# Weight chunks whose low part is made by an adding DMA instead of VectorE

## The chip, the cores and the metric

One core of one Trainium2 chip runs the kernel. The metric is the device time of one execution in microseconds (us).

## The reference

The reference is a two-layer decoder trunk on 256 tokens of width 2048, all in float32. Nearly all of its arithmetic lies in products with weight matrices. Layer 0 mixes tokens by causal spatial gating in parallel with attention into 256 memory tokens, layer 1 by latent attention in parallel with the same memory attention; each layer ends in a gated feed-forward block:

```python
D_MODEL = 2048; SEQ = 256; D_FF = 5632
...
for l in range(DEPTH):                      # DEPTH = 2
    h = rmsnorm(x, g_mix[l])
    ...                                     # main (gating or latent attention), mo (memory attention)
    x = x + jnp.concatenate([main, mo], axis=-1) @ w_out[l]
    x = x + conv_ffn(rmsnorm(x, g_ffn[l]), w_ffn_up[l], conv_w[l], conv_b[l], w_ffn_down[l])
return rmsnorm(x, g_final)

def conv_ffn(h, w_up, cw, cb, w_down):
    a = h @ w_up                            # 2048 x 11264
    ...                                     # causal depthwise convolution of width 3
    gate, val = c[..., :D_FF], c[..., D_FF:]
    return (jax.nn.silu(gate) * val) @ w_down
```

## The kernel before, in words

Every weight is read once from memory and used once. To keep float32 accuracy with a faster matmul type, each operand is split into a high part, which is the value rounded to that type (`F32R`), and a low part, which is the value minus its high part. A product is then high by high plus high by low plus low by high.

The weights come in *chunks*. `chunk` (line 92 on) allocates three tiles of 128 x 1024 values: `raw` (five buffers), `whi` and `wlo` (three each). SP issues the load of `raw` (line 98). For a chunk without gains ACT copies `raw` to `whi` (line 117) and DVE subtracts: `wlo = raw - whi` (line 118). Chunks with a per-row gain take lines 122 and 123, and other shapes lines 105/106 and 113/114. A full chunk holds two blocks of 128 rows by 512 columns of the weight, 512 KB.

`gemm_fm` makes four output blocks of 128 channels at a time, each accumulated in a PSUM bank (`ps`, eight banks, so two GEMMs' worth). It goes through the contraction two blocks at a time, one chunk each: 16 blocks make eight chunks, numbered 0 to 7 here. `mm_fm` issues a chunk's matmuls: eight of 512 columns with `whi` as weights (line 140; the moving operand holds the high and the low part of 256 tokens side by side) and eight of 256 columns with `wlo` (line 144). Even chunks do the high ones first, odd chunks the low ones first.

After a GEMM come its evictions. In the feed-forward block each of the four output blocks goes through `join` (ACT copies half the bank to `cr`, line 200; DVE adds it, `js`, line 202), POOL multiplies by the row factor (`a`, line 549), ACT and DVE do the convolution (`c`, lines 552 to 554) and ACT the gate (line 562) or DVE and ACT the product and its split. The next GEMM runs on the other four banks meanwhile. In the down-projection and the output projection DVE adds the two halves to the residual (lines 507 and 508).

The feed-forward block works in three parts of 4, 4 and 3 groups of 512 channels; a group is one GEMM of eight chunks for the gate and one for the value, and a part ends with four GEMMs of the down-projection, of eight, eight and six chunks. The order of the instructions on each engine is set when the program is built, by a scheduler that models a timeline; at run time each engine works through its own list in order and waits on semaphores.

Of the kernel before, what the change touches and what calls it, by code (L numbers as in the profile page):

```python
# [8 lines left out]
F32 = mybir.dt.float32  # L9
F32R = mybir.dt.float32r  # L10
I32 = mybir.dt.int32
BF16 = mybir.dt.bfloat16
AF = mybir.ActivationFunctionType
ALU = mybir.AluOpType
AX = mybir.AxisListType

P = 128
# [52 lines left out]
class Kernel:  # L70
# [18 lines left out]
        return pool.tile(shape, dt, tag=tag, name=self.uid(tag), bufs=bufs)  # L89


    def chunk(self, src, nk, ncol, gains=None, twice=False, heads=None):
        nc, n = self.nc, nk * ncol
        raw = self.wp.tile([P, 1024], F32, tag="raw", name=self.uid("raw"), bufs=5)
        hi = self.wp.tile([P, 1024], F32R, tag="whi", name=self.uid("whi"), bufs=3)
        lo = self.wp.tile([P, 1024], F32R, tag="wlo", name=self.uid("wlo"), bufs=3)
        view = lambda x: x[:, :n].rearrange("p (k c) -> p k c", k=nk)
        nc.sync.dma_start(out=view(raw), in_=src)
        if twice:
            both = lambda x: x.rearrange("p (k o c) -> p k o c", o=2, c=ncol)  # L100
            for k in range(nk):
                s = slice(k * ncol, (k + 1) * ncol)
                for o in range(2):
                    h = both(hi)[:, k, o, :]
                    nc.scalar.activation(h, raw[:, s], AF.Copy, scale=gains[k])
                    nc.vector.scalar_tensor_tensor(both(lo)[:, k, o, :], raw[:, s], gains[k], h.bitcast(F32), ALU.mult, ALU.subtract)  # L106
            return tuple(x.rearrange("p (k c) -> p k c", k=nk) for x in (hi, lo))
        if heads is not None:

            s = view(raw).rearrange("p k (h c) -> p k h c", h=2)  # L110
            for c0, c1 in ((0, heads), (heads, ncol // 2)):
                o = lambda x: view(x)[:, :, 2 * c0 : 2 * c1].rearrange("p k (h c) -> p k h c", h=2)
                nc.scalar.activation(o(hi), s[:, :, :, c0:c1], AF.Copy)
                nc.vector.tensor_tensor(o(lo), s[:, :, :, c0:c1], o(hi).bitcast(F32), ALU.subtract)
            return view(hi), view(lo)
        if gains is None:
            nc.scalar.activation(hi[:, :n], raw[:, :n], AF.Copy)  # L117
            nc.vector.tensor_tensor(lo[:, :n], raw[:, :n], hi[:, :n].bitcast(F32), ALU.subtract)  # L118
        else:
            for k in range(nk):  # L120
                s = slice(k * ncol, (k + 1) * ncol)
                nc.scalar.activation(hi[:, s], raw[:, s], AF.Copy, scale=gains[k])  # L122
                nc.vector.scalar_tensor_tensor(  # L123
                    lo[:, s], raw[:, s], gains[k], hi[:, s].bitcast(F32), ALU.mult, ALU.subtract
                )
        return view(hi), view(lo)
# [31 lines left out]
    def gemm_fm(self, src, kbs, nblk, rhs, evict, nk=2, gain=None, hooks={}):  # L158
        accs = [self.psum() for _ in range(nblk)]
        for c in range(0, len(kbs), nk):  # L160
            g = None if gain is None else [gain(kbs[c + i]) for i in range(nk)]
            hi, lo = self.chunk(src(kbs[c], nk), nk, nblk * P, g)
            jobs = []
            for b in range(nblk):
                cols = slice(b * P, (b + 1) * P)
                for i in range(nk):
                    kk = c + i
                    jobs.append((accs[b], hi[:, i, cols], lo[:, i, cols], rhs(kbs[kk]), kk == 0, kk == len(kbs) - 1))
            self.mm_fm(jobs, (c // nk) % 2)
            for f in hooks.get(c // nk, ()):  # L170
                f()
        for b in range(nblk):
            evict(b, accs[b])
# [135 lines left out]
    def gain(self, name, k):  # L309
        c = self.g[name] + k  # L310
        return self.gT[:, c : c + 1]
# [280 lines left out]
    def layer_a(self):  # L592
        nc, t, tc = self.nc, self.t, self.tc
# [3 lines left out]
        with ExitStack() as ctx:  # L597
# [25 lines left out]
            def spatial_weights():  # L623
                nc.sync.dma_start(out=bb, in_=t["b_sp"][0].rearrange("(o g) t -> o g t", o=1).to_broadcast([P, GH, P]))
                for g in range(0, GH, 4):
                    raw = self.wp.tile([P, 1024], F32, tag="raw", name=self.uid("raw"), bufs=5)
                    rv = raw[:, :512].rearrange("p (g s) -> p g s", g=4)
                    nc.sync.dma_start(out=rv, in_=t["w_sp"][0, g : g + 4].rearrange("g t s -> t g s"))
                    acc = self.psum()
                    for i in range(4):  # L630
                        nc.tensor.transpose(acc[:, i * P : (i + 1) * P], rv[:, i, :], self.ident)
                    for i in range(4):
                        nc.vector.tensor_tensor(wT[:, g + i, :], acc[:, i * P : (i + 1) * P], self.keep, ALU.mult)
# [329 lines left out]
```

## Time and profile before

| | |
|---|---|
| median of 2 runs | 2136.97 us (2136.78 to 2137.16) |
| the profiled execution | 2136.6 us, span 2134.5 us |
| mean granted TensorE clock | 0.997 |
| busy share of the span | PE 99%, PEld 87%, DVE 70%, ACT 54%, POOL 16% |
| DMA | 391 MB, 183 GB/s on average, 56.6% of 16 engines |

The span runs from the first to the last instruction of the profiled execution. PE is the matmul row and PEld the weight load that overlaps it; matmuls are pipelined and their ends are modelled, so a high share of PE doesn't say that it is at its peak. A line number names the line of the kernel that issued an instruction, and a tile is named by the program's name without its buffer number (`wlo`, `raw`). In the list of waits the columns are the waiting engine, tile and line, what ended the wait, the total in us, the number of waits and the longest.

### The profile page before, as it was taken

Reading aid. Unit: us, or ns where it says so; the run is one execution under the profiler, and the core shown is the slowest. Engines: PE = TensorE matmul, PEld = TensorE weight load, DVE = VectorE, ACT = ScalarE, POOL = GpSimd, SP = SyncE. Lnnn points to the kernel's source line nnn. Section 1 sums busy time; section 2 is a strip of 40 time slices with the busy share of each in tenths; the row PEclk is TensorE's granted clock in tenths of the full one; section 3 lists DMA queues with packets and bytes.
Section 4 is the critical chain, followed back from the end, with each engine's and each line's share of the span. In section 5 each row is a group of like instructions: output and inputs, shape, how many; then the busy total and the mean of one; then the engine's idle time right before and its main releaser. Section 6 shows DMA issues by size and latency. Waiting matters only on the chain.

```text
span 2134.5 us, 31965 instructions
## 1 busy us (share of the span) xinstructions
PE 2109.3 (99%) x11980; PEld 1847.7 (87%) x11980; DVE 1483.8 (70%) x2247; ACT 1151.5 (54%) x1800; POOL 338.3 (16%) x401
## 2 busy tenths in 40 slices
PE   8999999999999999999999999999999999999997
PEld 7888888888888888888888778888888888888886
DVE  6656667777656776667888775777765677656775
ACT  7654744656435564355556654465643556435554
POOL 0000124111001110011244111411100111001122
PEclk9999999999999999999999999999999999999998
DMA  8565455565555655566555523566555565556653
GB/s 280 179 206 183 154 193 188 188 194 182 196 188 188 191 184 194 187 190 190 186 188 164 155 97 129 188 188 194 182 196 188 188 191 184 196 187 189 189 187 109
DMA packets 208015, 391.02 MB, mean 183 GB/s; under 512 B 14366, under 2 KB 22900, under 8 KB 207860
## 3 DMA queue, kind: packets, MB, share of 16 engines
q1 hardware_dynamic: 207860, 388.98, 56.6%
q8 instruction: 94, 1.54, 0.3%
q14 instruction: 61, 0.50, 0.1%
HBM read 386.84 MB, written 2.10 MB: 182 GB/s over the span
## 4 chain that ended last, share of the span: by engine, by line
PE 97%; DVE 1%; ACT 1%; POOL 0%; DMA 0%; issue 0%; SPq 0%; ACTq 0%; DVEq 0%
PE ps L140 58%; PE ps L144 30%; PE ps L179 2%; PE ps L181 2%; PE ps L180 2%; PE ps L807 1%; PE ps L805 0%; PE ps L501 0%; PE ps L371 0%; PE ps L466 0%; PE ps L641 0%; DMA raw<-in_w_mem_kv 0%; DVE wlo L106 0%; PE ps L828 0%; PE ps L726 0%
## 5 line engine op out<-in xcount | busy, mean ns | idle before, releaser
L118 DVE TENSOR_TENSOR wlo<-raw,whi 128x1024 fp32r<-128x1024 f32 x660 | 820.6, 1245 | 484.7 <-ACT whi L117 480.6
L117 ACT ACTIVATE whi<-raw 128x1024 fp32r<-128x1024 f32 x660 | 697.6, 1057 | 647.6 <-PE ps L140 529.0
L140 PE MATMUL ps<-xhl,whi 128*128 128x512 f32 x3280 | 788.4, 391 | 1.6 <-ACT whi L122 1.6
L140 PEld LDWEIGHTS ps<-xhl,whi 128*128 128x128 f32 x3280 | 601.8, 188 | 117.4 <-ACT whi L122 1.8
L144 PEld LDWEIGHTS ps<-xhl,wlo 128*128 128x128 f32 x3280 | 422.9, 191 | 17.8 <-DVE wlo L106 0.7
L144 PE MATMUL ps<-xhl,wlo 128*128 128x256 f32 x3280 | 431.3, 283 | 0.2 <-DVE wlo L106 0.2
L549 POOL TENSOR_TENSOR a<-js,rbc 128x256 f32<-128x256 f32 x176 | 167.1, 960 | 1167.4 <-DVE js L202 1017.1
L140 PE MATMUL ps<-h,whi 128*128 128x512 f32 x1408 | 338.8, 391 | 0.0
L140 PEld LDWEIGHTS ps<-h,whi 128*128 128x128 f32 x1408 | 258.1, 188 | 49.5
L144 PEld LDWEIGHTS ps<-h,wlo 128*128 128x128 f32 x1408 | 181.4, 191 | 7.2
L144 PE MATMUL ps<-h,wlo 128*128 128x256 f32 x1408 | 184.7, 283 | 0.0
L552 ACT ACTIVATE c<-a,cT 128x256 f32<-128x256 f32 x176 | 99.9, 592 | 76.5 <-POOL a L549 76.5
L200 ACT ACTIVATE cr<-ps 128x256 f32<-128x256 f32 x243 | 91.0, 381 | 92.4 <-PE ps L140 83.4
L140 PE MATMUL ps<-mainhl,whi 128*128 128x512 f32 x512 | 122.7, 391 | 0.0
L202 DVE TENSOR_TENSOR js<-ps,cr 128x256 f32<-128x256 f32 x213 | 89.7, 422 | 43.9 <-ACT cr L200 23.7
L123 DVE SCALAR_TENSOR_TENSOR wlo<-raw,gT,whi 128x512 fp32r<-128x512 f32 x112 | 87.5, 820 | 32.6 <-ACT whi L122 30.1
L140 PEld LDWEIGHTS ps<-mainhl,whi 128*128 128x128 f32 x512 | 94.1, 188 | 18.2
L554 DVE SCALAR_TENSOR_TENSOR c<-a,cT,c 128x254 f32<-128x254 f32 x176 | 105.4, 599 | 1.6
L553 DVE SCALAR_TENSOR_TENSOR c<-a,cT,c 128x255 f32<-128x255 f32 x176 | 94.9, 560 | 9.8 <-ACT c L552 8.6
L122 ACT ACTIVATE whi<-raw,gT 128x512 fp32r<-128x512 f32 x112 | 74.8, 716 | 40.2 <-PE ps L140 16.6
L144 PEld LDWEIGHTS ps<-mainhl,wlo 128*128 128x128 f32 x512 | 65.7, 191 | 2.5
L144 PE MATMUL ps<-mainhl,wlo 128*128 128x256 f32 x512 | 66.4, 283 | 0.0
(236 smaller groups left out, 1474.9 us busy)
## 6 DMA issues: line engine op xcount, KB each, us to landing
raw<-in_w_ffn_up SPq DMA_DIRECT2D x352, 512.0 KB, 4.2
raw<-in_w_ffn_down SPq DMA_DIRECT2D x176, 512.0 KB, 4.4
raw<-in_w_out SPq DMA_DIRECT2D x64, 512.0 KB, 3.7
raw<-in_w_in_a SPq DMA_DIRECT2D x56, 512.0 KB, 3.5
raw<-in_w_mem_kv SPq DMA_DIRECT2D x32, 512.0 KB, 4.3
raw<-in_w_in_b SPq DMA_DIRECT2D x16, 512.0 KB, 4.1
raw<-in_w_uq SPq DMA_DIRECT2D x12, 384.0 KB, 3.5
raw<-in_w_kv_a SPq DMA_DIRECT2D x8, 512.0 KB, 4.3
```

The source lines that it names most:

```text
L117: nc.scalar.activation(hi[:, :n], raw[:, :n], AF.Copy)
L118: nc.vector.tensor_tensor(lo[:, :n], raw[:, :n], hi[:, :n].bitcast(F32), ALU.subtract)
L122: nc.scalar.activation(hi[:, s], raw[:, s], AF.Copy, scale=gains[k])
L123: nc.vector.scalar_tensor_tensor(lo[:, s], raw[:, s], gains[k], hi[:, s].bitcast(F32), ALU.mult, ALU.subtract)
L140: mm(acc[:, :], wh, x, start=first, stop=last)
L144: mm(acc[:, S:], wl, x[:, :S], start=False, stop=False)
L200: self.nc.scalar.activation(cr, acc[:, S:], AF.Copy)
L202: self.nc.vector.tensor_tensor(o, acc[:, :S], cr, ALU.add)
L549: nc.gpsimd.tensor_tensor(a, self.join(acc), rb, ALU.mult)
L552: nc.scalar.activation(c, a, AF.Identity, scale=w(2), bias=w(3))
L553: nc.vector.scalar_tensor_tensor(c[:, 1:], a[:, : S - 1], w(1), c[:, 1:], ALU.mult, ALU.add)
L554: nc.vector.scalar_tensor_tensor(c[:, 2:], a[:, : S - 2], w(0), c[:, 2:], ALU.mult, ALU.add)
```

## The change

For every chunk of 128 x 1024 values without gains whose index in its GEMM leaves 2 when divided by 4 (indices 2 and 6), ACT makes the negated high part in `wlo` as well as the high part in `whi`. Then POOL issues a DMA that reads the same chunk from memory a second time and adds it to `wlo`, which gives the low part. DVE's subtraction is left out for these chunks; the other chunks stay as they were. `raw` has four buffers instead of five, `wlo` four instead of three; `whi` keeps three.

```diff
-    def chunk(self, src, nk, ncol, gains=None, twice=False, heads=None):
+    def chunk(self, src, nk, ncol, gains=None, twice=False, heads=None, added=False):
...
-        raw = self.wp.tile([P, 1024], F32, tag="raw", name=self.uid("raw"), bufs=5)
+        raw = self.wp.tile([P, 1024], F32, tag="raw", name=self.uid("raw"), bufs=4)
         hi = self.wp.tile([P, 1024], F32R, tag="whi", name=self.uid("whi"), bufs=3)
-        lo = self.wp.tile([P, 1024], F32R, tag="wlo", name=self.uid("wlo"), bufs=3)
+        lo = self.wp.tile([P, 1024], F32R, tag="wlo", name=self.uid("wlo"), bufs=4)
...
-        if gains is None:
+        if gains is None and n == 1024 and added:
+
+            nc.scalar.activation(hi, raw, AF.Copy)
+            nc.scalar.activation(lo, raw, AF.Copy, scale=-1.0)
+            nc.gpsimd.dma_start(out=view(lo), in_=src, accum_op=ALU.add)
+        elif gains is None:
             nc.scalar.activation(hi[:, :n], raw[:, :n], AF.Copy)
             nc.vector.tensor_tensor(lo[:, :n], raw[:, :n], hi[:, :n].bitcast(F32), ALU.subtract)
...
-            hi, lo = self.chunk(src(kbs[c], nk), nk, nblk * P, g)
+            hi, lo = self.chunk(src(kbs[c], nk), nk, nblk * P, g, added=(c // nk) % 4 == 2)
```

The buffer count of `raw` is changed in the same way where the spatial weights are loaded.

More of the change, by code (lines that the diff above doesn't have):

```diff
@@ L625, in spatial_weights @@
                 for g in range(0, GH, 4):
-                    raw = self.wp.tile([P, 1024], F32, tag="raw", name=self.uid("raw"), bufs=5)
+                    raw = self.wp.tile([P, 1024], F32, tag="raw", name=self.uid("raw"), bufs=4)
                     rv = raw[:, :512].rearrange("p (g s) -> p g s", g=4)
```

## The prediction

> **What bounds the kernel now.** I read the page's busy shares first, then the chain that ended last, then PE's waits, then the stage windows.
>
> ```profile
> span 2134.5 us, 31965 instructions
> PE 2109.3 (99%) x11980; PEld 1847.7 (87%) x11980; DVE 1483.8 (70%) x2247; ACT 1151.5 (54%) x1800; POOL 338.3 (16%) x401
> q1 hardware_dynamic: 207860, 388.98, 56.6%
> PE 97%; DVE 1%; ACT 1%; POOL 0%; DMA 0%; issue 0%; SPq 0%; ACTq 0%; DVEq 0%
> L549 POOL TENSOR_TENSOR a<-js,rbc 128x256 f32<-128x256 f32 x176 | 167.1, 960 | 1167.4 <-DVE js L202 1017.1
> ...
> raw<-in_w_ffn_up SPq DMA_DIRECT2D x352, 512.0 KB, 4.2
> ```
>
> PE is busy for 2109.3 of 2134.5 us, and the chain that ended last runs 97% through it. DVE, whose work is reduced, idles 30% of the span. PE's waits, all of them:
>
> ```profile
> PE ps L294 <- DMA graw<-in_g_mem: 5.2, 1, 5.2
> PE ps L140 <- ACT whi L122: 2.5, 2, 1.6
> PE ps L917 <- ACT xg L912: 2.1, 4, 0.8
> PE ps L140 <- DVE qhl L213: 1.6, 1, 1.6
> PE ps L501 <- ACT pT L494: 0.9, 1, 0.9
> PE ps L726 <- POOL kr L743: 0.7, 1, 0.7
> PE ps L837 <- ACT pT L830: 0.6, 1, 0.6
> PE ps L490 <- DVE mp L482: 0.5, 1, 0.5
> PE ps L144 <- DVE wlo L106: 0.2, 1, 0.2
> ```
>
> They add up to 14.3 us, 2.3 of them on DVE and none on line 118, the subtraction that is to be replaced. So a faster DVE has about 2 us to give. Everything else the change can do is to make PE wait.
>
> The stage in which most of the changed chunks lie, by windows (PE, PEld, DVE, ACT, POOL busy, clock, DMA share, GB/s) and by a stretch of the timeline (start, duration):
>
> ```profile
> 500.00:1000.00 500.00, 500.00 (x2876) 441.93 (x2875) 341.69 (x479) 257.44 (x358) 57.02 (x60) 1.00 0.59 189
> 623.78 1.06 ACT L117 ACTIVATE whi<-raw 128x1024 fp32r<-128x1024 f32 x1 [2.69 <-PE ps L140]
> 624.87 1.23 DVE L118 TENSOR_TENSOR wlo<-raw,whi 128x1024 fp32r<-128x1024 f32 x1 [2.53 <-ACT whi L117]
> 625.39 2.08 PE L144 MATMUL ps<-h,wlo 128*128 128x256 f32 x16
> 625.59 1.06 ACT L117 ACTIVATE whi<-raw 128x1024 fp32r<-128x1024 f32 x1 [0.75 <-PE ps L140]
> 627.31 3.82 PE L140 MATMUL ps<-h,whi 128*128 128x512 f32 x16
> 629.35 1.06 ACT L117 ACTIVATE whi<-raw 128x1024 fp32r<-128x1024 f32 x1 [2.69 <-PE ps L140]
> 630.96 2.08 PE L144 MATMUL ps<-h,wlo 128*128 128x256 f32 x16
> 636.53 2.08 PE L144 MATMUL ps<-xhl,wlo 128*128 128x256 f32 x16
> ```
>
> An even chunk multiplies its high parts first and its low parts last, the odd chunk after it the other way round, so PE alternates 16 low and 16 high matmuls. A pair takes 630.96 - 625.39 = 5.57 us, a chunk 2.785 us: low parts (627.31 - 625.39) / 2 = 0.96, high parts 1.83. The clock is granted in full and PE is busy in all 500 us. ACT's `whi` begins 0.2 us after the high matmuls that free its buffer (625.39, then 625.59): ACT is paced by PE, three chunks ahead.
>
> **What is removed and added.** The program order of the changed kernel holds 152 added chunks, those with index 2 or 6 of a GEMM: 88 in ffn_up (44 GEMMs of eight chunks), 40 in ffn_down, 16 in w_out, 8 in w_in_a. The rows for one operation (minimum, median, maximum in ns):
>
> ```profile
> L117 ACT ACTIVATE whi<-raw x660: 1041/1060/1067, 102.1 to 2109.1; 128x1024 fp32r<-128x1024 f32 x165
> L118 DVE TENSOR_TENSOR wlo<-raw,whi x660: 1160/1226/1765, 103.2 to 2110.2; 128x1024 fp32r<-128x1024 f32 x165
> L98 SPq DMA_DIRECT2D raw<-in_w_ffn_up x352: 367/368/368, 351.5 to 2029.7; - x176
> DMA to landing us min/median/max: 3.3/4.2/7.8
> L242 POOL TENSOR_TENSOR ssum<-ssum,sq 128x256 f32<-128x256 f32 x45 | 55.2, 1227 | 1.9
> ```
>
> - DVE loses 152 x 1.226 = 186 us, ACT gains 152 x 1.060 = 161 us (1151.5 to about 1313). Both are hidden: before a negation ACT sat idle 0.75 or 2.69 us per chunk in the rows above. Worth on the path: 0.
> - 152 x 512 KB = 80 MB are read a second time, a fifth on top of q1's 389 MB. By bytes alone the engines' share rises from 0.59 to about 0.74 in the FFN. No bound yet.
> - `raw` goes from five buffers to four. A `raw` is free when its subtraction ends, 624.87 + 1.23 = 626.10. The load that reuses it lands 4.2 us later, at 630.3; its `whi` starts four chunks after 623.78, at 634.92. That leaves 4.6 us at the median landing, 1.0 at the longest (7.8). For an added chunk the release is the end of its second ACT operation (618.21 + 1.06 = 619.3, four chunks before 629.35) and the next use a negation at 626.65, so 3.1 us are left at the median. I take 0; if landings lengthen past 7 us this cover is gone, and a late negation is what comes next.
> - The wait. In the order of the changed program ACT does `whi` of the chunk before, then the negation, then the added chunk's own `whi`; POOL issues the adding DMA; PE's first low matmul of that chunk waits for the DMA. What is queued behind that wait is PE's whole remaining order, so each microsecond is paid in full.
>
> **The time that is there.** With four `wlo` buffers an added chunk reuses the buffer of the chunk four before it. Take the low matmuls at 625.39 as that chunk's: its buffer is free at 625.39 + 0.96 + 0.2 = 626.55. ACT ends `whi` at 625.59 + 1.06 = 626.65 and the negation at 627.71. Four chunks later the low matmuls start, at 636.53. There are **8.8 us** for an adding DMA.
>
> That holds where ACT does nothing else. Index 6 of an ffn_up GEMM falls behind the evictions of the GEMM before:
>
> ```profile
> 697.76 2.08 PE L144 MATMUL ps<-xhl,wlo 128*128 128x256 f32 x16
> 697.96 1.06 ACT L117 ACTIVATE whi<-raw 128x1024 fp32r<-128x1024 f32 x1 [0.70 <-PE ps L140]
> 699.67 3.82 PE L140 MATMUL ps<-xhl,whi 128*128 128x512 f32 x16
> 701.26 1.44 POOL L549 TENSOR_TENSOR a<-js,rbc 128x256 f32<-128x256 f32 x2 [15.04 <-DVE js L202]
> 705.46 1.22 DVE L118 TENSOR_TENSOR wlo<-raw,whi 128x1024 fp32r<-128x1024 f32 x1
> 708.89 2.08 PE L144 MATMUL ps<-xhl,wlo 128*128 128x256 f32 x16
> 711.38 0.42 ACT L562 ACTIVATE gate<-c 128x256 f32<-128x256 f32 x1 [0.46 <-DVE c L554]
> 720.03 2.08 PE L144 MATMUL ps<-xhl,wlo 128*128 128x256 f32 x16
> ```
>
> The GEMM begins at 699.67 + 1.83 = 701.5; the low matmuls of its indices 2 and 6 start at 708.89 and 720.03. For index 2 nothing changes: 697.96 + 1.06 + 1.06 = 700.08, 8.8 us left. For index 6 the changed order puts both last gates, one `whi` and then the negation: 711.38 + 0.42 + 2 x 1.06 = 713.92, **6.1 us** left. The chain of evictions waits for DVE; where one subtraction of 1.22 less stands in it, 7.3 us are left. I take the middle, **6.7 us**, for 44 chunks. In ffn_down the eviction is two DVE additions, so its chunks keep 8.8, and I count the other 108 chunks so.
>
> **The price of an adding DMA.** No row shows one, nor POOL issuing any. From the rows of a load: it lands in 4.2 us, of which the engines work 0.59 x 2.785 = 1.64; 2.56 are the rest. An add reads the chunk and also the tile that it adds to, so its engine time lies between 1.64 (a load's) and 6.56 (four loads'), and I take two loads', 3.28, for the two reads. It shares the engines with loads that work 0.59 of the time. Alone it would need 3.28; at half speed whenever a load is there, 3.28 / (0.41 + 0.59 x 0.5) = 4.65. POOL's issue lies between SP's 0.37 and POOL's dearest operation, 1.23; I take 1.23, since POOL's mean `a` (0.96) already takes more than twice SP's issue. So 1.23 + 2.56 + 4.65 = **8.4 us**, with ends at 0.37 + 2.56 + 1.64 = 4.6 and, were a load in the way throughout and taking half, 1.23 + 2.56 + 3.28 / 0.5 = 10.35.
>
> The Trainium skill, Collectives: The Full Stack, section The bandwidth ceiling, says the add in a DMA costs no time of its own but needs two source reads on one ring, measured as 1.93 times a copy. By that the engine time is 3.17, the total 8.3 us; no run here shows it yet.
>
> **The sum.** Index 2 and the others: 8.4 is under 8.8, nothing. Index 6 in ffn_up: 8.4 - 6.7 = 1.7 us late, 44 times, 75 us. A stall moves all that follows by its length, and the next added chunk starts from its own freed buffer, so stalls add. The profiled run took 2136.6 us, 2.1 more than its span, and lies 0.4 below the median of the two runs shown, 2136.97. 2136.6 + 75 = **2212 us**, 3.5% slower. About 2% (43 us) is what a measurement of this kernel tells from no change; that is a stall of 1.0 us in each of the 44.
>
> **The rivals.**
> 1. *Hidden anyway, not slower.* The place is the same wait of PE. If the issue is SP's 0.37 and the add mostly has the engines to itself, 0.37 + 2.56 + 3.28 = 6.2 us, under the 6.7 of index 6. Up to 7.7 us (44 stalls of 1.0) it stays within 2%. The time is 2136.6, less at most the 2.3 us that PE waited for DVE: about 2137. For it: DMA engines idle 41% of the stage. Against it: loads occupy the rest, and the add is in flight for longer than a load's whole interval of 2.785. The Trainium skill, DMA: Bandwidth & Descriptors, section Anatomy of one DMA, fits a DMA issued by GpSimd as 2.0 us plus bytes over 436 GB/s; taken twice for two reads, an estimate of 4.4 us, which would be hidden. No run here shows it.
> 2. *POOL's queue blocks.* The DMA of index 2 issues at 700.08 and POOL's first `a` begins at 701.26, 1.2 us later. If an issue holds POOL for 2.5 us (twice 1.23), every eviction is 1.3 later, `js` (two buffers) holds up DVE, index 6 has 6.7 - 1.3 = 5.4 us, and the DMA takes 2.5 + 2.56 + 4.65 = 9.7. That is 44 x 4.3 + 108 x 0.9 = 286 us: 2423. For it: 176 `a` operations stand on this path; against: 1.2 us is a long issue beside 0.37.
> 3. *The add is dear.* At four loads' engine time: 1.23 + 2.56 + 6.56 / 0.705 = 13.1 us, 108 x 4.3 + 44 x 6.4 = 746 us: 2883. Against: nothing in the rows asks for four.
> 4. *DVE's relief brings over 2%.* PE's waits on DVE are 2.3 us in all; it would take PE's matmuls themselves to run faster, and the rows show full clock.
>
> **How the numbers follow.** Forecast 0.46; hidden 0.38; POOL 0.07; dear 0.07; over 2% faster 0.02. So slower 0.60, same 0.38, faster 0.02. The forecast's own range is 2180 (7.7 us) to 2470: at 10.35 us the stalls are 44 x 3.65 + 108 x 1.55 = 328. The range takes in the hidden case, 2132 (PE's DVE waits gone and a little beside) and ends at 2480; what lies above is the dear case and part of POOL's.
>
> **What would show it.** Right: PE's waits list a DMA writing `wlo`, with about 44 to 60 waits of 1 to 2 us, at index 6 of ffn_up; DVE falls to about 1298, ACT rises to about 1313; landings of `raw` rise from 4.2 to 5 or 6. Hidden: no such wait, and `wlo` landing within 7 us. POOL: issue rows over 2 us and `a` starting late after the DMA. Dear: index 2 and ffn_down stall as well, by 4 us. The forecast is wrong if PE waits instead for `whi` (loads or ACT late), or if PE's busy time itself changes.

## The result, and the profile after

The changed kernel takes **2225.27 us** (median of two runs, 2222.95 to 2227.59) against 2136.97 before: 1.0411 times as long, with a 95% interval of [1.0386, 1.0436]. It is slower by 88 us. The profiled execution took 2227.59 us over a span of 2225.9, 91.4 us more than the span before.

First the page of the changed kernel, in the order in which it was read before: busy shares, DMA queues, the chain that ended last (here it could be followed back over 46% of the span), POOL's `a`, and the adding DMAs with their median time from issue to landing.

```profile
span 2225.9 us, 32291 instructions
PE 2139.3 (96%) x11980; PEld 1849.0 (83%) x11980; DVE 1305.9 (59%) x2095; ACT 1307.6 (59%) x1952; POOL 525.3 (24%) x553
q1 hardware_dynamic: 207860, 388.98, 55.8%
q0 software_dynamic: 41344, 79.70, 21.0%
PE 24%; DMA 12%; ACT 5%; issue 2%; DVE 2%; POOL 1%; ACTq 0%; DVEq 0%; POOLq 0%
L554 POOL TENSOR_TENSOR a<-js,rbc 128x256 f32<-128x256 f32 x176 | 187.5, 1126 | 96.9 <-ACT whi L122 95.1
...
wlo<-in_w_ffn_up POOLq DMA_DIRECT2D x88, 512.0 KB, 8.3
wlo<-in_w_ffn_down POOLq DMA_DIRECT2D x40, 512.0 KB, 8.7
wlo<-in_w_out POOLq DMA_DIRECT2D x16, 512.0 KB, 8.8
```

DVE is relieved by 1483.8 - 1305.9 = 178 us and ACT loaded with 1307.6 - 1151.5 = 156, as the change says. The chain, 97% PE before, now has DMA as its second largest part. A piece of it in order of time, from w_out, shows how (start, length):

```profile
1364.95 1.23 PE ps L149 x8
1366.20 1.07 ACT wlo L119
1367.56 8.98 DMA wlo<-in_w_out
1376.59 2.17 PE ps L149 x16
```

Low matmuls end and free a buffer, ACT negates into it, the DMA takes 8.98 us from its issue, and the next low matmuls that it serves start when it has landed. PE's high matmuls are off the chain in that time.

PE's waits (what ended the wait, total in us, number, longest):

```profile
PE ps L149 <- DMA wlo<-in_w_ffn_up: 31.2, 37, 2.1
PE ps L149 <- DMA wlo<-in_w_ffn_down: 18.1, 19, 2.6
PE ps L149 <- DMA wlo<-in_w_in_a: 6.3, 2, 5.4
PE ps L299 <- DMA graw<-in_g_mem: 5.5, 1, 5.5
PE ps L149 <- DMA wlo<-in_w_out: 4.5, 7, 1.4
```

Four rows are new: the low matmuls (line 149 now) wait for the adding DMA in 65 places, 60.1 us in all. The wait for `graw` was there before (5.2). PE's own busy time has grown by 2139.3 - 2109.3 = 30.0 us; its ends are modelled, so part of a pause can stand there as work, and part of the matmuls ran at half clock (below). 60.1 + 30.0 = 90.1 is nearly the whole growth of 91.4.

One such wait in the timeline of the changed kernel, at index 6 of an ffn_up GEMM (start, duration; in brackets the idle time before and what ended it):

```profile
715.15 2.07 PE L149 MATMUL ps<-xhl,wlo 128*128 128x256 f32 x16
716.25 1.05 ACT L122 ACTIVATE whi<-raw 128x1024 fp32r<-128x1024 f32 x1
717.50 1.05 ACT L119 ACTIVATE wlo<-raw 128x1024 fp32r<-128x1024 f32 x1
718.85 1.20 POOL L120 DMA_DIRECT2D wlo<-in_w_ffn_up  x1 [4.98 <-ACT wlo L119]
722.62 3.81 PE L145 MATMUL ps<-xhl,whi 128*128 128x512 f32 x16
727.68 2.18 PE L149 MATMUL ps<-xhl,wlo 128*128 128x256 f32 x16 [1.24 <-DMA wlo<-in_w_ffn_up]
```

ACT ends the negation at 717.50 + 1.05 = 718.55; POOL starts the DMA 0.30 us later and is held for 1.20. Sixteen high matmuls take 3.65 us from start to start of what follows where nothing waits (627.31 to 630.96 in the rows of before), so the low ones were due at 722.62 + 3.65 = 726.27, 7.7 us after the negation's end. They start at 727.68, 9.1 us after that: 1.4 us late.

The same reckoning for all chunks tells how the loss is spread. For each chunk the time from the start of the matmul before to the start of a low matmul, summed over its eight low matmuls, was taken in both traces and subtracted:

```
lateness (us)            index 2   index 6
ffn_up    (44 and 44)        5.0      39.4
ffn_down  (24 and 16)       11.7      13.2
w_out      (8 and 8)         3.5       3.0
w_in_a     (4 and 4)         6.3       1.0
sum                         26.5      56.6
```

That is 83 of the 91.4 us, and 23 more than the waits of 60.1: the rest of these pauses, and the slower matmuls behind some of them, stand in PE's busy time.

### The profile page after: what moved, and what is told of

Its sections match the earlier page's. It is cut to its first block, busy times and chain, and to the rows that moved or that the text cites. A ratio compares the mean times of both kernels' runs of the same rounds, so it can differ in the third digit from the quotient of the medians.

```text
span 2225.9 us, 32291 instructions
## 1 busy us (share of the span) xinstructions
PE 2139.3 (96%) x11980; PEld 1849.0 (83%) x11980; DVE 1305.9 (59%) x2095; ACT 1307.6 (59%) x1952; POOL 525.3 (24%) x553
## 5 line engine op out<-in xcount | busy, mean ns | idle before, releaser
L123 DVE TENSOR_TENSOR wlo<-raw,whi 128x1024 fp32r<-128x1024 f32 x508 | 646.3, 1272 | 634.8 <-ACT whi L122 634.2
L122 ACT ACTIVATE whi<-raw 128x1024 fp32r<-128x1024 f32 x508 | 536.0, 1055 | 489.2 <-PE ps L145 368.1
L149 PE MATMUL ps<-xhl,wlo 128*128 128x256 f32 x3280 | 438.8, 286 | 37.9 <-DMA wlo<-in_w_ffn_up 31.2
L120 POOL DMA_DIRECT2D wlo<-in_w_ffn_up x88 | 105.6, 1200 | 665.1 <-ACT wlo L119 665.1
L554 POOL TENSOR_TENSOR a<-js,rbc 128x256 f32<-128x256 f32 x176 | 187.5, 1126 | 96.9 <-ACT whi L122 95.1
L149 PE MATMUL ps<-h,wlo 128*128 128x256 f32 x1408 | 189.8, 287 | 18.2 <-DMA wlo<-in_w_ffn_down 18.1
L119 ACT ACTIVATE wlo<-raw 128x1024 fp32r<-128x1024 f32 x152 | 159.9, 1052 | 45.2 <-PE ps L149 44.0
L120 POOL DMA_DIRECT2D wlo<-in_w_ffn_down x40 | 48.0, 1199 | 392.2 <-ACT wlo L119 381.8
```

What stands on the lines that cost most here:

```text
L119: nc.scalar.activation(lo, raw, AF.Copy, scale=-1.0)
L120: nc.gpsimd.dma_start(out=view(lo), in_=src, accum_op=ALU.add)
L149: mm(acc[:, S:], wl, x[:, :S], start=False, stop=False)
L554: nc.gpsimd.tensor_tensor(a, self.join(acc), rb, ALU.mult)
```

## The experiments

Two theories of why PE waits. *W*: the price of an adding DMA, from the end of the negation to its landing, is longer than the time that the chunk's low matmuls leave it; its rivals were that something else that came with the change costs the time (`raw`'s lost buffer, POOL's queue, the doubled reading). *O*, on where that time comes from: ACT's list. The negation stands behind the `whi` of the chunk before, which waits for one of three `whi` buffers, so it can't start earlier however many `wlo` buffers there are; its rival was that the count of `wlo` buffers sets it. A time without an interval is that of one run.

**The buffers alone.** The kernel before, with the change's buffer counts and nothing else:

```diff
-        raw = self.wp.tile([P, 1024], F32, tag="raw", name=self.uid("raw"), bufs=5)
+        raw = self.wp.tile([P, 1024], F32, tag="raw", name=self.uid("raw"), bufs=4)
...
-        lo = self.wp.tile([P, 1024], F32R, tag="wlo", name=self.uid("wlo"), bufs=3)
+        lo = self.wp.tile([P, 1024], F32R, tag="wlo", name=self.uid("wlo"), bufs=4)
```

> The kernel before with the new buffer counts alone: raw 4 instead of 5, wlo 4 instead of 3, no chunk added by DMA. Theory W (PE waits for the adding DMA, which takes longer than the 8.8 us between the negation and the low matmuls): the buffer counts cost nothing, 2137 us within 5. Rival R (loads come late because raw has one buffer less): a good part of the 88 us is already here, over 2160 us, and ACT waits for raw loads.

2137.61 us, 1.0002 times before [0.9992, 1.0012]. The lost `raw` buffer costs nothing where no chunk is added.

**Half of the chunks: index 2, then index 6.** The changed kernel with one of the two indices left to the DMA.

```diff
-            hi, lo = self.chunk(src(kbs[c], nk), nk, nblk * P, g, added=(c // nk) % 4 == 2)
+            hi, lo = self.chunk(src(kbs[c], nk), nk, nblk * P, g, added=(c // nk) % 8 == 2)   # or == 6
```

> The changed kernel with only index 2 of each GEMM added (80 chunks instead of 152). In the changed kernel's trace the low matmuls of index 2 start 26 us late in sum, those of index 6 57 us. Theory W with independent chunks: 2137 + 26 = 2163 us at most, and less where fewer adds share the DMA engines, so 2145 to 2163. Rival R: the loss doesn't follow the index, half of it or more stays, 2180 or more.

> The changed kernel with only index 6 of each GEMM added (72 chunks). Theory W: up to 57 us, 2170 to 2194, with most of the waits in ffn_up, where the negation stands behind the evictions on ACT. Rival (the place of the negation does not matter, each add costs the same): 72/152 of 88 us, 2179 with waits spread evenly over ffn_up and ffn_down.

Index 2 alone (80 chunks) takes 2187.78 us, index 6 alone (72) 2197.67. Index 2 was expected to cost at most 26 us and costs 51. Index 6 alone costs 61 us, 4 more than the top of what was expected. The same tally of lateness gives 59 us for index 6 alone, as in the changed kernel (57), but 48 for index 2 alone against 26.5. Most of that difference is in ffn_down (about 26 against 11.7), where the adds of index 2 land later when they are alone; landings and PE's waits of the index-2 kernel:

```profile
wlo<-in_w_ffn_up POOLq DMA_DIRECT2D x44, 512.0 KB, 8.5
wlo<-in_w_ffn_down POOLq DMA_DIRECT2D x24, 512.0 KB, 9.6
...
PE ps L149 <- DMA wlo<-in_w_ffn_down: 19.9, 20, 1.7
```

Median 9.6 us in place of 8.7. So the two losses don't add up (51 + 61 = 112 against 88). Between the first and the last packet of an add of ffn_down, loads here move 1.9 chunks' worth of bytes by the packet records, against 1.45 in the changed kernel; that the add competes with more loads fits, but no run separates it from other causes.

**A copy in place of the add.** Everything else stays: the same 80 MB are read again, by the same queue and into the same tile; what is left out is the reading and adding of what `wlo` held.

```diff
-            nc.gpsimd.dma_start(out=view(lo), in_=src, accum_op=ALU.add)
+            nc.gpsimd.dma_start(out=view(lo), in_=src)
```

> The changed kernel with a plain copy in place of the adding DMA: the same 152 transfers from POOL, of the same bytes into the same tiles, but the old contents of wlo are not read and added, so the low parts hold the chunk itself and the output is not the reference's. Theory W with the price as predicted (an add is two loads' engine time, 3.28 us instead of 1.64, stretched by the sharing): the landing falls by about 2.3 us from 8.3 to about 6, the waits of PE go, 2137 to 2150 us. Rival I (what costs is that POOL issues the DMA, and the second read of the weights): the landing stays over 7.5 us and the time over 2190.

2157.92 us (2154.90 to 2160.19), 1.0096 times before [1.0081, 1.0112]: 21 us remain of the 88. Its queue, POOL's issue (minimum, median, maximum in ns), the landings of all its copies in us, and PE's waits:

```profile
q0 software_dynamic: 41344, 79.70, 12.2%
L120 POOL DMA_DIRECT2D wlo<-in_w_ffn_up x88: 716/716/762, 370.4 to 2056.3; - x88
DMA to landing us min/median/max: 4.7/6.7/9.7
PE ps L149 <- DMA wlo<-in_w_ffn_down: 7.4, 4, 2.4
PE ps L149 <- DMA wlo<-in_w_ffn_up: 2.2, 3, 1.0
```

The wait goes with the add's own price, as W says: 67 us are bought with 1.6 us of landing (8.3 to 6.7), 0.48 of them in POOL's issue. The result lies above the expected 2137 to 2150: the copy lands at 6.7 where about 6 was expected, and its longest take 9.7. By the tally 9.5 us of what is left lie at four chunks, index 6 of the first ffn_down GEMM of each part, where copies landed after 8.6 to 9.7 us and 7.4 to 7.7 us were there. The bytes alone don't explain the slowdown.

**Five `wlo` buffers.** To make room, `junk` of layer 0 uses `bb`, `u` has one buffer and `p` three.

```diff
-        lo = self.wp.tile([P, 1024], F32R, tag="wlo", name=self.uid("wlo"), bufs=4)
+        lo = self.wp.tile([P, 1024], F32R, tag="wlo", name=self.uid("wlo"), bufs=5)
```

> The changed kernel with five wlo buffers instead of four (to make room, one scratch tile of layer 0 shares the tile of the spatial biases, u has one buffer instead of two, p three instead of four). In ACT's order the negation still stands behind the whi of the chunk before, which waits for one of three whi buffers. Theory O (ACT's order sets when the negation can start): in the trace of before that whi ends at 626.65 and the fourth wlo buffer is free at 626.55, so a fifth gains 0.1 us at most, 2215 to 2235. Rival B (the count of wlo buffers sets it): 2.8 us more slack, waits gone, 2137 to 2150.

2223.1 us: a fifth buffer changes nothing, as O says. In the changed kernel the negation did wait for its buffer:

```profile
ACT wlo L119 <- PE ps L149: 44.0, 61, 2.6
```

With five buffers this row is gone from ACT's waits, yet PE waits as before:

```profile
ACT whi L122 <- PE ps L145: 368.7, 252, 3.6
...
PE ps L149 <- DMA wlo<-in_w_ffn_up: 35.0, 36, 2.4
PE ps L149 <- DMA wlo<-in_w_ffn_down: 12.9, 15, 2.3
```

The wait of `whi` for its buffers was there before (368.1 us in the changed kernel) and has not grown. But from the negation's end to the time at which the low matmuls are due, the added chunks of ffn_up and ffn_down gain 0.2 us at most in the mean, near the 0.1 that was expected. So with four buffers the free buffer and ACT's list hold the negation at about the same time, and one more buffer alone gives nothing. An earlier place in the list without the fifth buffer was not tried.

**Three `wlo` buffers** (and five of `raw`), which takes time away from the DMA.

```diff
-        raw = self.wp.tile([P, 1024], F32, tag="raw", name=self.uid("raw"), bufs=4)
+        raw = self.wp.tile([P, 1024], F32, tag="raw", name=self.uid("raw"), bufs=5)
-        lo = self.wp.tile([P, 1024], F32R, tag="wlo", name=self.uid("wlo"), bufs=4)
+        lo = self.wp.tile([P, 1024], F32R, tag="wlo", name=self.uid("wlo"), bufs=3)
```

> The changed kernel with three wlo and five raw buffers, as before the change. The negation must wait for the low matmuls of the chunk three before: free at 627.31 + 0.2 in the trace of before, negation done at 628.57, low matmuls at 636.53, so 7.96 us instead of 8.8 for the 108 chunks that do not stand behind evictions. If the landing stays as it is, each of these waits up to 0.85 longer, 90 us: about 2315. If a waiting PE also stops the loads and so shortens the landing, half of that: about 2270. If buffers do not matter: 2225.

2325.03 us, near the 2315 expected for a landing that stays as it is, but partly by luck. The 90 us were expected at the 108 chunks that do not stand behind evictions. By the tally these lose 80 us where they lost 44, and index 6 of ffn_up, which was left out, loses 84 where it lost 39; the mean clock also falls, from 0.992 to 0.983. The adds still land at 8.2, though PE and its loads are now held up more:

```profile
PE ps L149 <- DMA wlo<-in_w_ffn_up: 82.7, 54, 3.5
PE ps L149 <- DMA wlo<-in_w_ffn_down: 36.7, 23, 3.3
...
wlo<-in_w_ffn_up POOLq DMA_DIRECT2D x88, 512.0 KB, 8.2
```

**The odd chunks** (indices 1 and 5; 160 adds, since the GEMMs of six chunks have both). Their low matmuls come first in the chunk, so the DMA has less time.

```diff
-            hi, lo = self.chunk(src(kbs[c], nk), nk, nblk * P, g, added=(c // nk) % 4 == 2)
+            hi, lo = self.chunk(src(kbs[c], nk), nk, nblk * P, g, added=(c // nk) % 4 == 1)
```

> The changed kernel with the chunks of index 1 and 5 added instead of 2 and 6. An odd chunk needs its low part first: in the trace of before the whi ahead of the negation starts at 629.35, the negation ends at 631.5 and the low matmuls start at 626.35 + 11.14 = 637.49, 6.0 us instead of 8.8. With the landing as in the changed kernel (8.3 to 8.8, and 0.3 from the negation to the issue) each of 152 chunks waits 2.7 to 3.0 us: about 2560. If a waiting PE stops the loads, and the add finds the DMA engines free, the landing falls to 7.3 to 7.8 and the time lies at 2370 to 2450. If only the number of adds counts, 2225.

2764.65 us, beyond the 2560 expected. PE's waits, the landing, and the window of the FFN stage (PE, PEld, DVE, ACT, POOL busy, granted clock, DMA share, GB/s):

```profile
PE ps L149 <- DMA wlo<-in_w_ffn_up: 253.0, 86, 4.8
PE ps L149 <- DMA wlo<-in_w_ffn_down: 127.0, 43, 4.4
...
wlo<-in_w_ffn_up POOLq DMA_DIRECT2D x88, 512.0 KB, 8.3
...
500.00:1000.00 500.00, 401.13 (x2130) 347.03 (x2128) 220.80 (x330) 228.13 (x317) 86.29 (x83) 0.95 0.64 175
```

The waits for `wlo` (253.0 and 127.0 above, 62.3 in w_out and w_in_a) come to 442 us, near the 423 that a time of 2560 stands for. The landing is 8.3 once more, though the engines are less busy (0.64 against 0.82 in the changed kernel). Of the other 186 of the 628 us a lower clock can explain most: its mean over the span is 0.943, so (1 - 0.943) x 2 x 2762.7 = 315 us ran at half clock, some 300 more than before, which cost up to about 150. The rest isn't accounted for.

**The added chunk's preparation moved ahead.** On top of the fifth `wlo` buffer, the load, the negation and the DMA of an added chunk are issued before the chunk ahead of it is prepared (`early`); its `whi` follows in its old place (`late`).

```diff
+    def early(self, src):
...
+        nc.sync.dma_start(out=view(raw), in_=src)
+        nc.scalar.activation(lo, raw, AF.Copy, scale=-1.0)
+        nc.gpsimd.dma_start(out=view(lo), in_=src, accum_op=ALU.add)
+        return raw, lo
...
+            if full and (c // nk) % 4 == 1 and c + nk < len(kbs):
+                pre = self.early(src(kbs[c + nk], nk))
+            if full and (c // nk) % 4 == 2:
+                hi, lo = self.late(*pre)
+            else:
+                hi, lo = self.chunk(src(kbs[c], nk), nk, nblk * P, g)
```

> As the run with five wlo buffers, but the load, the negation and the adding DMA of an added chunk are issued ahead of the chunk before it, so that the negation stands in ACT's order before that chunk's whi. The fifth buffer is then free early, the negation ends at 625.9 in the trace of before and 10.6 us are there instead of 8.8; in ffn_up at index 6 about 1 us more than in the changed kernel. Theory W with O: most waits go, 2137 to 2155, all 152 adds still done. Rival (the adds cost through the DMA engines' share, ACT's or POOL's work, whatever the place of the wait): over 2190.

2177.73 us, 1.0204 times before [1.0181, 1.0227]; the expected 2137 to 2155 was missed. Half of the loss is gone, and with it every wait of index 2, of w_out and of w_in_a. What stays in PE's waits, and the largest wait of ACT for a load:

```profile
PE ps L165 <- DMA wlo<-in_w_ffn_up: 20.5, 16, 2.3
PE ps L165 <- DMA wlo<-in_w_ffn_down: 10.4, 4, 3.2
...
ACT wlo L98 <- DMA raw<-in_w_ffn_up: 31.7, 25, 2.8
```

By the tally these are index 6 of 16 ffn_up GEMMs, those behind the evictions of a value GEMM, and index 6 of a part's first ffn_down GEMM; they hold 37 of the 41 us that are left. In the program's order there the scheduler still has ACT do the negation after the `whi` of the chunk before, so the kernel didn't do there what it was made for. ACT also waits for late loads of `raw`, more than the 24.3 us of the changed kernel in that row, but none of these waits stands directly before the negation of one of the 20 late chunks.

**The same with index 2 alone** (80 adds): `% 8` in place of `% 4` in both conditions.

> As the early run, with index 2 of each GEMM alone (80 adds): in the early run no low matmul of index 2 was late. Theory W with O (an add costs nothing where the time from its negation to its low matmuls is longer than its landing, whatever it does to DMA, ACT and POOL): 2136 to 2142. Rival (something of the adds' cost remains on the path, or the waits move to index 2 when index 6 no longer waits, as they did when index 2 was added alone without the hoist): over 2150. And if DVE's relief by 80 subtractions were worth something, it would show here as under 2133.

2136.62 us, 0.9998 times before [0.9989, 1.0008]. Busy shares, the landings in ffn_up and ffn_down, and the one wait for an add of ffn_down that is left:

```profile
PE 2109.1 (99%) x11980; PEld 1846.5 (86%) x11980; DVE 1405.0 (66%) x2167; ACT 1224.4 (57%) x1880; POOL 434.4 (20%) x481
...
wlo<-in_w_ffn_up POOLq DMA_DIRECT2D x44, 512.0 KB, 6.8
wlo<-in_w_ffn_down POOLq DMA_DIRECT2D x24, 512.0 KB, 9.2
...
PE ps L165 <- DMA wlo<-in_w_ffn_down: 0.7, 1, 0.7
```

In ffn_down, where index 2 alone lost most, the adds are nearly as slow as then (9.2 us against 9.6) and yet hidden, since 10.7 us are there instead of 8.9: the same 80 chunks cost 51 us when their negation came later. That shows W, and with the fifth buffer alone at no gain it shows O there. In ffn_up the adds also land sooner, at 6.8 us against 8.5, so for these 44 chunks the earlier place and the shorter landing work together. The run also shows what a hidden add is worth: DVE has 1483.8 - 1405.0 = 79 us less to do, and the time is that of before.

**Half of each chunk.** The DMA adds the second block of 256 KB; DVE subtracts the first.

```diff
-            nc.scalar.activation(lo, raw, AF.Copy, scale=-1.0)
-            nc.gpsimd.dma_start(out=view(lo), in_=src, accum_op=ALU.add)
+            nc.scalar.activation(lo[:, 512:], raw[:, 512:], AF.Copy, scale=-1.0)
+            nc.vector.tensor_tensor(lo[:, :512], raw[:, :512], hi[:, :512].bitcast(F32), ALU.subtract)
+            nc.gpsimd.dma_start(out=view(lo)[:, 1, :], in_=src[:, 1, :], accum_op=ALU.add)
```

> The changed kernel with half of each added chunk: the DMA adds the second 128 rows of the chunk's two blocks (256 KB), DVE subtracts for the first. Price by parts, from the changed kernel's trace: 0.3 from the negation to the issue, first packet 2.8 after the issue, 1.5 of engine time stretched by the loads to 2.6, 0.35 to the landing: 6.1 us instead of 8.6 to 9.1. Theory W: under 6.7 nearly everywhere, 2137 to 2150. Rival (the fixed part of the price, POOL's issue and what follows it, is most of it): the landing stays over 7.3 us, and the time over 2180.

2138.44 us, 1.0006 times before [0.9996, 1.0015], as expected. The landings of all its adds, and POOL's issue:

```profile
L121 POOL DMA_DIRECT2D wlo<-in_w_ffn_up x88: 856/870/889, 368.1 to 2039.6; - x88
DMA to landing us min/median/max: 4.3/6.0/7.4
```

The longest landing is 7.4 us, which with the 0.30 before it makes 7.7. At index 6 of ffn_up and ffn_down 8.0 us or more are there, some of it because the negation of half a chunk takes 0.62 instead of 1.05 us.

**Two DMAs of 256 KB in place of one.**

```diff
-            nc.gpsimd.dma_start(out=view(lo), in_=src, accum_op=ALU.add)
+            for k in range(nk):
+                nc.gpsimd.dma_start(out=view(lo)[:, k, :], in_=src[:, k, :], accum_op=ALU.add)
```

> The changed kernel with each adding DMA split into two of 256 KB, issued one after the other by POOL, same bytes. If an issue holds POOL for a fixed 1.2 us, the second half starts 1.2 later; the first half's packets run meanwhile, so the landing of the second is later by 0 to 1.2 us, and POOL is held for 2.4, past the 1.2 us that it has before the evictions of the next GEMM: 2225 plus up to 150, 2240 to 2375. If the issue takes time by its size (0.6 each), nothing changes: 2215 to 2235.

2205.1 us, outside both expectations: faster than one DMA of 512 KB, though POOL is held twice.

```profile
L121 POOL DMA_DIRECT2D wlo<-in_w_ffn_up x176: 856/958/1241, 375.3 to 2104.6; - x176
wlo<-in_w_ffn_up POOLq DMA_DIRECT2D x176, 256.0 KB, 6.9
```

So POOL's queue isn't what costs the time. By the packet records the first packet moves 1.9 us after the start of the first issue, against 2.8 with one DMA, and the last ends after 7.5 against 8.0. It is one run, and the kernel still takes 68 us more than before.

No version was faster than the kernel before; the two that hide the adds are equal to it.

## Why the prediction was right, and where two of its terms were wrong

The time came out at 2225, where 2212 was forecast, and the mechanism is the one named: PE waits for the adding DMA, and everything behind it moves by that much. The copy, the shorter add and the earlier negation each take the waits away, fewer buffers and the odd chunks add to them. But the near hit of the sum is partly luck, since two of its terms erred in opposite directions: 75 us at index 6 of ffn_up were 39, and nothing at the other chunks was 44. One of its own signs of being wrong also came: PE's busy time rose by 30 us. By the tally most of that belongs to the same pauses, so it names no other cause.

- **What bounds the kernel, and what DVE's relief is worth.** Nothing, as costed: index 2 prepared early takes 79 us off DVE for 0.9998 times the time. DVE ended at 1306 and ACT at 1308 us, by rows that forecast 1298 and 1313. The rival of a gain over 2% falls.
- **`raw` with four buffers.** Costed at nothing; 1.0002 [0.9992, 1.0012] alone. In the changed kernel ACT's `whi` waits 24.3 us for late loads of ffn_up, in 17 places, so the cover is thinner there; PE waits only 3.1 us for `whi` itself. Five `raw` buffers beside the adds and four `wlo` were not run. The rows show no landing for these loads, so their forecast 5 to 6 us can't be compared.
- **The price, 8.4 us.** Landings were 8.3, 8.7 and 8.8 in ffn_up, ffn_down and w_out (7.5 in the eight of w_in_a), but the 0.30 us between ACT's end and POOL's start was left out: the price is 8.6 to 9.1 in these three. Its parts were near: issue 1.20 (1.23 forecast), engine time 21.0% x 2225.9 / 152 = 3.08 us (3.28). The Trainium skill, Collectives: The Full Stack, section The bandwidth ceiling, has an all-gather, which copies, 1.93 times as fast as a reduce-scatter, which adds. Here the copy takes 12.2% x 2153.2 / 152 = 1.73 us, so the traces show 1.78 for this DMA. By the fit in the Trainium skill, DMA: Bandwidth & Descriptors, section Anatomy of one DMA, the estimate was 4.4 us. The measured 8.3, in a stage where the engines are busy to 0.82, decides against it.
- **The 108 chunks counted at nothing.** This is the term that failed: they lose 83 - 39 = 44 us. Where nothing else holds ACT up, the time there is 8.9 us, much as costed, but the price has a spread: its median is 8.4 at index 2 of ffn_up and about 9.0 in ffn_down and w_out, and single adds reach 10.7. So 27 us go in many small waits; a margin of 0.4 us between two estimates, one of them made of three assumed terms, should have carried a cost in the sum. Another 10 us go at four chunks, index 6 of the first ffn_down GEMM of each part: these stand behind the evictions of ffn_up, which the prediction left out for ffn_down, and have 7.4 to 8.5 us. And 6 us go at one chunk of w_in_a, whose low matmuls were due 5.0 us after the negation's end while its add landed after 10.0.
- **Index 6 of ffn_up, 1.7 us each.** It pays 39.4 / 44 = 0.9 us, 39 in place of 75. From the negation's end to the time at which the low matmuls were due, the trace has 8.2 us in the mean of the 44, not 6.7, and more than even the upper end of 7.3; the price at index 6 is 8.9 in the mean. Behind gate evictions, which the prediction worked out, 22 GEMMs have 8.2 us and lose 16 in all; behind the evictions of a value GEMM, as in the timeline above, 16 have 7.8 and lose 23; six that open a part have 9.0 and lose 1. The step that was off is the place of the evictions: the last gate ends 0.9 us after the low matmuls of index 2 start (median of the 22), where the rows of before have 711.38 + 0.42 - 708.89 = 2.9. With the buffer counts alone it ends at 2.9 too, with index 2 alone at 0.9, with index 6 alone at 3.3. So the evictions come through 2 us earlier where DVE is spared the subtraction of index 2; the prediction had allowed 1.2 at most. With index 6 alone 8.2 us are there all the same, because the program's order then has the negation ahead of the last gate: the scheduler's order counts as well.
- **"Stalls add."** They don't: 51 and 61 us alone, 88 together. With both indices added the adds of ffn_down land sooner (8.7 against 9.6 us), beside fewer loads; why there are fewer is open.
- **POOL's queue.** An issue takes 1.20, not 2.5 us. `a` got longer (mean 0.96 to 1.13 us), yet two issues a chunk were faster than one. The rival falls.
- **Hidden anyway.** It would have needed 7.7 us or less. The copy at 6.7 comes within 1% of it, the half chunk at 6.0 reaches it. The 2% that the prediction takes for what a measurement can tell is too coarse: the intervals above reach 0.1 to 0.3% to each side. The rival's mechanism was sound and its price too low by 2 us.

## What to carry to other kernels

Price a transfer from the end of what it needs to its landing, under the traffic that will be there, and hold it against the time that the engines' in-order lists leave it, stage by stage; a margin of a few tenths of a microsecond is a cost, not a cover. When the margin is missing, look for what starts the transfer late: here an earlier place in the list, with the buffer that it needs, was worth 51 us, and the buffer alone nothing. Work taken from an engine that isn't the bound buys nothing even when it is perfectly hidden, and puts a new wait on the engine that is.

## What the runs showed of the hardware that had not been expected

**The clock can halve after short pauses.** Three windows of the changed kernel: the FFN stage, and two stretches around a wait of PE for an adding DMA.

```profile
500.00:1000.00 500.00, 481.25 (x2700) 418.43 (x2700) 269.73 (x397) 281.08 (x367) 107.23 (x96) 0.99 0.82 222
588.20:591.40 3.20, 3.20 (x15) 3.01 (x14) 1.23 (x1) 1.15 (x2) 1.16 (x1) 0.50 0.66 230
871.50:878.10 6.60, 6.06 (x22) 5.57 (x23) 2.18 (x4) 2.11 (x2) 1.20 (x1) 0.50 0.70 228
```

The granted clock, 1.00 in all of the FFN stage before, is 0.50 in the last two. The record of the clock has five such stretches ahead of the tail, of 3.41 or 6.83 us, 23.9 us in all, which cost up to 12 us; four of them follow pauses of 2.2 to 3.0 us between starts of matmuls, one a pause of 5.7. Not every such pause has one: after pauses of 2.5 and 2.6 us in the same run the clock stayed full. Before, and in the two kernels that hide the adds, there is none until the tail. The odd chunks, with a mean clock of 0.943, lost up to about 150 us to it. The Trainium skill, TensorE: Matmul & The Clock Gate, section Part 1: The HAM clock gate (the "warmup" mystery), puts the clock at half after an idle window of about 3.4 us. The stretches here, of one or two times 3.41 us, agree with such a window, but pauses of 2.2 to 3.0 us were enough.

**What an add meets is not the stage's share.** In ffn_up the landing was 8.3 us in a stage with a DMA share of 0.82, and 8.3 with the odd chunks at 0.64, where PE waits longer and loads less. But these shares are means over the stage. By the packet records, between an add's first and last packet the loads took 0.42 of the engines in the changed kernel and 0.39 with the odd chunks (medians in ffn_up), nearly the same. With index 2 prepared early it was 0.27, and the landing 6.8 us. In ffn_down it was 0.39, 0.43 and 0.50 for landings of 8.7, 9.2 and 9.6 us (the changed kernel, index 2 early, index 2 alone). Within each stage the landing goes with the loads beside the add; that they cause it was not tried by itself, and the two stages differ by something else too.
